# Column sums of a matrix on one core: the last 256 rows loaded as two one-row blocks, fewer matmuls, and every store issued from SyncE

## The chip, the cores and the metric

The kernel runs on one core of a Trainium2 chip. The metric is the device time of one execution in microseconds (us). The profile's span is about 1.9 us shorter than that time.

## The reference

```python
def setup_inputs():
    return {"x": np.random.randn(8192, 8192).astype(np.float32)}

def reference(x):
    return np.sum(x, axis=0)
```

## The kernel before

Pairs of rows, one pair to a partition, stream through three buffers of 64 KB per partition. VectorE adds row a and then row b of each pair to a running sum. The last two blocks of 256 rows are not added by VectorE: TensorE sums them over partitions with a matmul against ones, and adds the running sum in the same PSUM tiles. The last block comes in five column strips, so that little is left to do once the last bytes land.

```python
STRIPS = [[(2048, 4), (2048, 4)], [(2048, 4)], [(1024, 4)], [(512, 4)], [(512, 4)]]
...
    for t in range(n_blocks - 2):                       # 30 pairs
        xt = load_pool.tile([P, K, C], F32, tag="xt")
        nc.sync.dma_start(out=xt, in_=xr[t])
        a, b = xt[:, 0], xt[:, 1]
        if prev is not None:
            nc.vector.tensor_tensor(out=a, in0=a, in1=prev[:, 1], op=ADD)   # L81
        nc.vector.tensor_tensor(out=b, in0=b, in1=a, op=ADD)                # L82
        prev = xt
    ...   # near: a whole block; last: the block in five strips, two rows per partition
    for piece in pieces:
        column_sums(prev[:, 1], piece, True, False)
    for piece in pieces:
        for k in range(K):
            column_sums(near[:, k], piece, False, False)
    for piece in pieces:                                # each piece has its own PSUM tile
        s, c0, w, nj, n, ps, res = piece
        for k in range(K):
            column_sums(last[:, k], piece, False, k == K - 1)
        rows = 32 * nj
        nc.vector.tensor_copy(out=res[0:rows, :], in_=ps[0:rows, :])
        eng = nc.scalar if s == len(STRIPS) - 1 else nc.sync    # last store: ScalarE's queue
        eng.dma_start(out=..., in_=res[0 : 32 * (nj - 1) + 1 : 32, :])
```

Of the kernel before, what the change touches and what calls it, by code (L numbers as in the profile page):

```python
# [1 line left out]

# [4 lines left out]

F32 = mybir.dt.float32
ADD = mybir.AluOpType.add





STRIPS = [
    [(2048, 4), (2048, 4)],
    [(2048, 4)],
    [(1024, 4)],
    [(512, 4)],
    [(512, 4)],  # L20
]


@with_exitstack
def kernel(
    ctx: ExitStack,
    tc: tile.TileContext,
    x: bass.AP,
    out: bass.AP,
):  # L30
    nc = tc.nc
    P = nc.NUM_PARTITIONS
    R, C = x.shape
    K = 2
    assert R % (P * K) == 0
    assert sum(w for s in STRIPS for w, _ in s) == C
    n_blocks = R // (P * K)

    xr = x.rearrange("(b p k) c -> b p k c", p=P, k=K)

    const_pool = ctx.enter_context(tc.tile_pool(name="const", bufs=1))
    load_pool = ctx.enter_context(tc.tile_pool(name="loads", bufs=3))
    psum_pool = ctx.enter_context(
        tc.tile_pool(name="psum", bufs=1, space=bass.MemoryType.PSUM)
    )

    ones = const_pool.tile([P, 32], F32)
    nc.gpsimd.memset(ones, 1.0)  # L48

    pieces = []  # L50
    c0 = 0
    for s, strip in enumerate(STRIPS):
        for w, nj in strip:
            n = w // nj
            i = len(pieces)
            ps = psum_pool.tile([P, n], F32, name=f"ps{i}", tag=f"ps{i}")
            res = const_pool.tile([P, n], F32, name=f"res{i}", tag=f"res{i}")
            pieces.append((s, c0, w, nj, n, ps, res))
            c0 += w

    def column_sums(src, piece, start, stop):
        _, c0, w, nj, n, ps, _ = piece
        for j in range(nj):
            nc.tensor.matmul(  # L64
                out=ps[32 * j : 32 * j + 32, :],
                lhsT=ones,
                rhs=src[:, c0 + j * n : c0 + (j + 1) * n],
                start=start,
                stop=stop,
                skip_group_check=True,  # L70
            )



    prev = None
    for t in range(n_blocks - 2):
        xt = load_pool.tile([P, K, C], F32, tag="xt")
        nc.sync.dma_start(out=xt, in_=xr[t])  # L78
        a, b = xt[:, 0], xt[:, 1]
        if prev is not None:  # L80
            nc.vector.tensor_tensor(out=a, in0=a, in1=prev[:, 1], op=ADD)  # L81
        nc.vector.tensor_tensor(out=b, in0=b, in1=a, op=ADD)  # L82
        prev = xt


    near = load_pool.tile([P, K, C], F32, tag="xt")
    nc.sync.dma_start(out=near, in_=xr[n_blocks - 2])
    last = load_pool.tile([P, K, C], F32, tag="xt")
    t = n_blocks - 1
    c = 0  # L90
    for strip in STRIPS:
        w = sum(w for w, _ in strip)
        nc.sync.dma_start(out=last[:, :, c : c + w], in_=xr[t][:, :, c : c + w])  # L93
        c += w

    for piece in pieces:
        column_sums(prev[:, 1], piece, True, False)
    for piece in pieces:
        for k in range(K):
            column_sums(near[:, k], piece, False, False)  # L100
    for piece in pieces:
        s, c0, w, nj, n, ps, res = piece
        for k in range(K):
            column_sums(last[:, k], piece, False, k == K - 1)
        rows = 32 * nj
        nc.vector.tensor_copy(out=res[0:rows, :], in_=ps[0:rows, :])  # L106
        eng = nc.scalar if s == len(STRIPS) - 1 else nc.sync
        eng.dma_start(
            out=out[c0 : c0 + w].rearrange("(j i) -> j i", j=nj),
            in_=res[0 : 32 * (nj - 1) + 1 : 32, :],  # L110
        )


# [1 line left out]
_INS = ['x']  # L115
_OUTS = [((8192,), 'float32')]


# [23 lines left out]
```

## Time and profile before

| quantity | value | where it is read |
|---|---|---|
| time, median of 9 runs of one session | 629.1 us (628.85 to 629.36) | the runs |
| DMA engines busy with loads and stores | 99.1% of the span | page, DMA queues |
| one pair of rows (8.389 MB) | 19.31 us, 434 GB/s | timeline, from one first add to the next |
| VectorE's two adds of a pair | 2 x 8.69 us, then 1.89 us idle for data | timeline |
| end of the last copy to end of the span | 2.6 us | timeline |

These lines are from the page of the kernel before: the span, each engine's busy time, and the DMA queue that carries loads and stores with its packets, MB and share.

```profile
span 626.8 us, 698 instructions
PE 21.1 (3%) x240; PEld 7.8 (1%) x240; DVE 515.9 (82%) x65; POOL 0.3 (0%) x5
q1 hardware_dynamic: 5864, 268.47, 99.1%
```

The next lines are from the timeline of the kernel before. Columns are start, duration, engine, line, operation, out<-in, shapes and count; the bracket gives the engine's idle time before it and what ended it. An engine name with a q is a sequencer that issues a DMA.

```profile
573.04 8.69 DVE L82 TENSOR_TENSOR xt<-xt 128x8192 f32<-128x8192 f32 x1
583.63 8.69 DVE L81 TENSOR_TENSOR xt<-xt 128x8192 f32<-128x8192 f32 x1 [1.89 <-DMA xt<-in_x_dram]
592.35 8.69 DVE L82 TENSOR_TENSOR xt<-xt 128x8192 f32<-128x8192 f32 x1
601.15 6.54 PE L64 MATMUL ps<-xt,ones 128*32 128x512 f32 x48 [601.15 <-DVE xt L82]
...
622.26 0.51 SPq L108 DMA_DIRECT2D out_dram<-res  x1
622.93 0.50 SPq L108 DMA_DIRECT2D out_dram<-res  x1
623.17 0.64 PE L64 MATMUL ps<-last,ones 128*32 128x128 f32 x16 [0.62 <-DMA last<-in_x_dram]
623.88 0.29 DVE L106 COPY res<-ps 128x128 f32<-128x128 f32 x1 [0.98 <-PE ps L64]
624.20 1.08 ACTq L108 DMA_DIRECT2D out_dram<-res  x1
```

VectorE waits about 1.89 us for data in every pair from the third on (10.70 us in the second, at 41.93), so the DMA stream is the bound until the loads end. After that there is a chain: the last data, matmuls (0.64 us; a matmul is recorded as two passes), copy (0.29 us), and the store's issue (1.08 us on ScalarE's queue), its landing and the final waits.

### The profile page before, as it was taken

Reading aid. Unit: us, or ns where it says so; the run is one execution under the profiler, and the core shown is the slowest. Engines: PE = TensorE matmul, PEld = TensorE weight load, DVE = VectorE, ACT = ScalarE, POOL = GpSimd, SP = SyncE. Lnnn points to the kernel's source line nnn. Section 1 sums busy time; section 2 is a strip of 40 time slices with the busy share of each in tenths; the row PEclk is TensorE's granted clock in tenths of the full one; section 3 lists DMA queues with packets and bytes.
Section 4 is the critical chain, followed back from the end, with each engine's and each line's share of the span. In section 5 each row is a group of like instructions: output and inputs, shape, how many; then the busy total and the mean of one; then the engine's idle time right before and its main releaser. Section 6 shows DMA issues by size and latency. Waiting matters only on the chain.

```text
span 626.8 us, 698 instructions
## 1 busy us (share of the span) xinstructions
PE 21.1 (3%) x240; PEld 7.8 (1%) x240; DVE 515.9 (82%) x65; POOL 0.3 (0%) x5
## 2 busy tenths in 40 slices
PE   0000000000000000000000000000000000000067
PEld 0000000000000000000000000000000000000022
DVE  0538988889988889888898888988889988889831
POOL 0000000000000000000000000000000000000000
PEclk9999999999999999999999999999999999999999
DMA  9999999999999999999999999999999999999996
GB/s 402 406 464 402 468 402 468 402 468 402 468 402 468 402 468 402 468 402 468 402 468 402 468 402 468 402 461 410 448 422 435 435 422 448 422 448 422 448 400 273
DMA packets 5876, 268.52 MB, mean 428 GB/s; under 512 B 600, under 2 KB 612, under 8 KB 1392
## 3 DMA queue, kind: packets, MB, share of 16 engines
q1 hardware_dynamic: 5864, 268.47, 99.1%
q8 instruction: 2, 0.03, 0.0%
q14 instruction: 2, 0.02, 0.0%
q10 hardware_dynamic: 8, 0.00, 0.0%
HBM read 268.44 MB, written 0.03 MB: 428 GB/s over the span
## 4 chain that ended last, share of the span: by engine, by line
DMA 78%; DVE 21%; SPq 0%; issue 0%; PE 0%; DVEq 0%
DMA xt<-in_x_dram 73%; DVE xt L81 21%; DMA last<-in_x_dram 4%; SPq L93 0%; PE ps L64 0%; SPq L78 0%; DVEq L81 0%; DVE res L106 0%
## 5 line engine op out<-in xcount | busy, mean ns | idle before, releaser
L81 DVE TENSOR_TENSOR xt<-xt 128x8192 f32<-128x8192 f32 x29 | 252.1, 8692 | 64.7 <-DMA xt<-in_x_dram 64.7
L82 DVE TENSOR_TENSOR xt<-xt 128x8192 f32<-128x8192 f32 x30 | 260.7, 8692 | 23.5 <-DMA xt<-in_x_dram 22.5
L64 PE MATMUL ps<-xt,ones 128*32 128x512 f32 (+2 forms) x48 | 6.5, 719 | 601.1 <-DVE xt L82 601.1
L106 DVE COPY res<-ps 128x512 f32<-128x512 f32 (+2 forms) x6 | 3.1, 514 | 20.0 <-PE ps L64 20.0
L64 PEld LDWEIGHTS ps<-xt,ones 128*32 128x32 f32 x48 | 2.1, 154 | 605.3 <-issue 605.3
L64 PE MATMUL ps<-last,ones 128*32 128x512 f32 (+2 forms) x96 | 7.9, 454 | 1.5 <-DMA last<-in_x_dram 1.5
L64 PE MATMUL ps<-near,ones 128*32 128x512 f32 (+2 forms) x96 | 7.1, 450 | 0.0
L64 PEld LDWEIGHTS ps<-near,ones 128*32 128x32 f32 x96 | 3.0, 110 | 3.9 <-issue 3.5
L64 PEld LDWEIGHTS ps<-last,ones 128*32 128x32 f32 x96 | 2.6, 109 | 6.6 <-DMA last<-in_x_dram 4.1
L48 POOL MEMSET ones<- 128x32 f32 x1 | 0.1, 125 | 0.3 <-POOLq L126 0.3
L126 POOL MEMSET const-bfloat16-1.0<- 128x1 bf16 x1 | 0.1, 102 | 0.0
L126 POOL MEMSET const-uint8-127<- 128x1 uint8 x1 | 0.1, 102 | 0.0
L126 POOL MEMSET const-float32-0.0<- 128x1 f32 x1 | 0.1, 99 | 0.2 <-issue 0.2
L126 POOL MEMSET const-float32-1.0<- 128x1 f32 x1 | 0.1, 99 | 0.0
## 6 DMA issues: line engine op xcount, KB each, us to landing
last<-in_x_dram SPq DMA_DIRECT2D x1, 4096.0 KB
last<-in_x_dram SPq DMA_DIRECT2D x1, 2048.0 KB
last<-in_x_dram SPq DMA_DIRECT2D x1, 1024.0 KB
last<-in_x_dram SPq DMA_DIRECT2D x2, 512.0 KB, 27.8
xt<-in_x_dram SPq DMA_DIRECT2D x30, 29.8
out_dram<-res SPq DMA_DIRECT2D x3, 8.0 KB
near<-in_x_dram SPq DMA_DIRECT2D x1
out_dram<-res SPq DMA_DIRECT2D x1, 4.0 KB
```

The lines of the kernel that those rows point to most:

```text
L48: nc.gpsimd.memset(ones, 1.0)
L64: nc.tensor.matmul(out=ps[32 * j : 32 * j + 32, :], lhsT=ones, rhs=src[:, c0 + j * n : c0 + (j + 1) * n], start=start, stop=stop, skip_gro ...
L81: nc.vector.tensor_tensor(out=a, in0=a, in1=prev[:, 1], op=ADD)
L82: nc.vector.tensor_tensor(out=b, in0=b, in1=a, op=ADD)
L106: nc.vector.tensor_copy(out=res[0:rows, :], in_=ps[0:rows, :])
L126: nc = _bacc.Bacc("TRN2", target_bir_lowering=False, num_devices=1)
```

## The change

The intent is a shorter end: the last 256 rows become two blocks of one row per partition, the first added by VectorE (for three quarters of the columns), the second in strips. Each strip then has half the descriptors and half the matmuls, and the slower issue on ScalarE's queue (1.08 us in the trace of before, against 0.50 to 0.66 on SyncE's) is avoided. In the built program, 60 matmuls are left of 120 (the page counts two passes each).

```diff
-STRIPS = [[(2048, 4), (2048, 4)], [(2048, 4)], [(1024, 4)], [(512, 4)], [(512, 4)]]
+GROUP = 2048
+NQ, NJ, NI = 4, 4, 128
+STRIPS = [8, 4, 2, 1, 1]                       # in units of 512 columns
...
+    ps = [psum_pool.tile([P, 512], F32, ...) for g in range(n_groups)]    # 4 PSUM tiles
...
+    def finish(eng_copy, u0, nu):
+        g, q = divmod(u0, NQ)
+        words = slice(NI * q, NI * (q + nu))
+        eng_copy(out=res[g][:, words], in_=ps[g][:, words])
+        nc.sync.dma_start(out=outr[:, u0 : u0 + nu], in_=res[g][...])
...
+    for t in range(n_pairs):                   # 31 pairs; the last one's row b is not added
...
+    nc.sync.dma_start(out=near, in_=xn)        # one row per partition
+    for nu in STRIPS:                          # one row per partition, in strips
+        nc.sync.dma_start(out=last[...], in_=xl[...])
...
+    for g in range(n_groups):
+        column_sums(prev[:, 1], g * NQ, NQ, True, False)
+    g = n_groups - 1
+    column_sums(prev[:, 0], g * NQ, NQ, False, False)
+    for g in range(n_groups - 1):              # VectorE: near += row a of the last pair
+        nc.vector.tensor_tensor(out=near[:, cols], in0=near[:, cols], in1=prev[:, 0, cols], op=ADD)
+    g = n_groups - 1
+    column_sums(near, g * NQ, NQ, False, False)
+    for g in range(n_groups - 1):
+        column_sums(near, g * NQ, NQ, False, False)
+        column_sums(last, g * NQ, NQ, False, True)
+        finish(nc.scalar.copy, g * NQ, NQ)
+    u = sum(STRIPS[:2])
+    for nu in STRIPS[2:]:                      # three strips, all in PSUM tile 3
+        column_sums(last, u, nu, False, True)
+        finish(nc.vector.tensor_copy, u, nu)
+        u += nu
```

More of the change, by code (lines that the diff above doesn't have):

```diff
@@ L9 @@
 ADD = mybir.AluOpType.add
-STRIPS = [
-    [(2048, 4), (2048, 4)],
-    [(2048, 4)],
-    [(1024, 4)],
-    [(512, 4)],
-    [(512, 4)],
-]
+GROUP = 2048
+NQ, NJ, NI = 4, 4, 128
+STRIPS = [8, 4, 2, 1, 1]
 @with_exitstack
@@ L33 @@
     R, C = x.shape
-    K = 2
-    assert R % (P * K) == 0
-    assert sum(w for s in STRIPS for w, _ in s) == C
-    n_blocks = R // (P * K)
-    xr = x.rearrange("(b p k) c -> b p k c", p=P, k=K)
+    assert R % (2 * P) == 0 and C == 512 * sum(STRIPS)
+    n_pairs = R // (2 * P) - 1
+    n_groups = C // GROUP
+    xp = x[: n_pairs * 2 * P].rearrange("(b p k) c -> b p k c", p=P, k=2)
+    xn = x[n_pairs * 2 * P : R - P]
+    xl = x[R - P :]
+    outr = out.rearrange("(u j i) -> j u i", j=NJ, i=NI)
     const_pool = ctx.enter_context(tc.tile_pool(name="const", bufs=1))
@@ L48, with column_sums @@
     nc.gpsimd.memset(ones, 1.0)
-    pieces = []
-    c0 = 0
-    for s, strip in enumerate(STRIPS):
-        for w, nj in strip:
-            n = w // nj
-            i = len(pieces)
-            ps = psum_pool.tile([P, n], F32, name=f"ps{i}", tag=f"ps{i}")
-            res = const_pool.tile([P, n], F32, name=f"res{i}", tag=f"res{i}")
-            pieces.append((s, c0, w, nj, n, ps, res))
-            c0 += w
-    def column_sums(src, piece, start, stop):
-        _, c0, w, nj, n, ps, _ = piece
-        for j in range(nj):
+    ps = [
+        psum_pool.tile([P, 512], F32, name=f"ps{g}", tag=f"ps{g}") for g in range(n_groups)
+    ]
+    res = [
+        const_pool.tile([P, 512], F32, name=f"res{g}", tag=f"res{g}") for g in range(n_groups)
+    ]
+    def column_sums(row, u0, nu, start, stop):
+        g, q = divmod(u0, NQ)
+        v = row[:, u0 * 512 : (u0 + nu) * 512].rearrange("p (q j i) -> p j q i", j=NJ, i=NI)
+        for j in range(NJ):
             nc.tensor.matmul(
-                out=ps[32 * j : 32 * j + 32, :],
+                out=ps[g][32 * j : 32 * j + 32, NI * q : NI * (q + nu)],
                 lhsT=ones,
-                rhs=src[:, c0 + j * n : c0 + (j + 1) * n],
+                rhs=v[:, j],
                 start=start,
@@ L71, in column_sums @@
             )
+    def finish(eng_copy, u0, nu):
+        g, q = divmod(u0, NQ)
+        words = slice(NI * q, NI * (q + nu))
+        eng_copy(out=res[g][:, words], in_=ps[g][:, words])
+        nc.sync.dma_start(
+            out=outr[:, u0 : u0 + nu],
+            in_=res[g][0 : 32 * (NJ - 1) + 1 : 32, words].rearrange("j (u i) -> j u i", i=NI),
+        )
     prev = None
-    for t in range(n_blocks - 2):
-        xt = load_pool.tile([P, K, C], F32, tag="xt")
-        nc.sync.dma_start(out=xt, in_=xr[t])
+    for t in range(n_pairs):
+        xt = load_pool.tile([P, 2, C], F32, tag="xt")
+        nc.sync.dma_start(out=xt, in_=xp[t])
         a, b = xt[:, 0], xt[:, 1]
@@ L81 @@
             nc.vector.tensor_tensor(out=a, in0=a, in1=prev[:, 1], op=ADD)
-        nc.vector.tensor_tensor(out=b, in0=b, in1=a, op=ADD)
+        if t < n_pairs - 1:
+            nc.vector.tensor_tensor(out=b, in0=b, in1=a, op=ADD)
         prev = xt
-    near = load_pool.tile([P, K, C], F32, tag="xt")
-    nc.sync.dma_start(out=near, in_=xr[n_blocks - 2])
-    last = load_pool.tile([P, K, C], F32, tag="xt")
-    t = n_blocks - 1
-    c = 0
-    for strip in STRIPS:
-        w = sum(w for w, _ in strip)
-        nc.sync.dma_start(out=last[:, :, c : c + w], in_=xr[t][:, :, c : c + w])
-        c += w
-    for piece in pieces:
-        column_sums(prev[:, 1], piece, True, False)
-    for piece in pieces:
-        for k in range(K):
-            column_sums(near[:, k], piece, False, False)
-    for piece in pieces:
-        s, c0, w, nj, n, ps, res = piece
-        for k in range(K):
-            column_sums(last[:, k], piece, False, k == K - 1)
-        rows = 32 * nj
-        nc.vector.tensor_copy(out=res[0:rows, :], in_=ps[0:rows, :])
-        eng = nc.scalar if s == len(STRIPS) - 1 else nc.sync
-        eng.dma_start(
-            out=out[c0 : c0 + w].rearrange("(j i) -> j i", j=nj),
-            in_=res[0 : 32 * (nj - 1) + 1 : 32, :],
-        )
+    tail = load_pool.tile([P, 2, C], F32, tag="xt")
+    near, last = tail[:, 0], tail[:, 1]
+    nc.sync.dma_start(out=near, in_=xn)
+    u = 0
+    for nu in STRIPS:
+        nc.sync.dma_start(
+            out=last[:, u * 512 : (u + nu) * 512], in_=xl[:, u * 512 : (u + nu) * 512]
+        )
+        u += nu
[4 more added lines that the diff above has]
+    for g in range(n_groups - 1):
+        cols = slice(g * GROUP, (g + 1) * GROUP)
+        nc.vector.tensor_tensor(
+            out=near[:, cols], in0=near[:, cols], in1=prev[:, 0, cols], op=ADD
+        )
+    g = n_groups - 1
[8 more added lines that the diff above has]
+        finish(nc.vector.tensor_copy, u, nu)
+        u += nu
 _INS = ['x']
```

## The prediction

> **What bounds it now.** The page shows the DMA engines 99.1% busy, VectorE 82%, TensorE 3%. In the timeline the two adds of a pair take 2 x 8.69 us, then VectorE waits 1.89 us for data: one pair per 19.31 us, 8.389 MB / 19.31 us = 434 GB/s. [...] Buffers come free about 10 us before the queue would run dry. So about 617 of 626.8 us of span are a stream that the change leaves alone. Only the end can move.
>
> **The end before.** Timeline: last data reaches TensorE at 623.17; 8 matmuls (16 passes, 128 wide) to 623.88; copy 0.29; store issued on ScalarE's queue 624.20 to 625.28 (1.08 us); its packets are done at 625.53; span 626.77. Stores on SyncE take 0.50 to 0.66 us to issue.
>
> **Removed.** (a) Half the descriptors of the last 8 MB. Packets took 611 ns for 16 KB, 309 for 8, 159 for 4, 84 for 2: some 8 ns each beyond bytes. Estimated per engine: 19.73 us instead of 20.0, so data end 0.27 us earlier. (b) Four of eight matmuls of each strip: about 0.2 us. (c) Last store on SyncE: issue to data done 0.6 us instead of 1.33: 0.7 us.
>
> **Added.** (d) The last three strips share one PSUM tile, and the built program makes each strip's matmuls wait for VectorE's copy of the strip before: a series. Estimated from durations of before: matmuls 4x256 to copy 0.71, copy 0.42, matmuls 4x128 0.50, copy 0.29, matmuls 0.50, copy 0.29, handovers 0.12: 2.83 us from the first strip's start. (e) VectorE's add of pair 30 (602.9 to 611.6), then three 2048-column adds once the one-row block lands (612.7), estimated 2.29 us each, ending 615.0, 617.4, 619.7. TensorE then has near and last of groups 1 and 2, 0.86 us a group of four 512-wide matmuls at full clock, and reaches the strips at about 621.75, when the 1024-column strip lands (621.4 to 621.7). (f) ScalarE's copies and table load: off the path.
>
> **Sum.** 621.75 + 2.83 = 624.58 end of last copy, against 624.17; the SyncE store is done at 625.2, against 625.53. Gains of 1.2 us are mostly eaten by (d). Span about 626.45, time **628.7 us**, range **628.1 to 629.7**. Chance of faster by over 2%: 0.005; within 2%: 0.985; slower by over 2%: 0.01. (2% is 12.6 us, more than the tail.)
>
> **What would show it.** Timeline of the end: first matmul at 602.9, released by DMA, no longer VectorE; TensorE idle about 609 to 611.6; TensorE waiting for VectorE's copies between the last strips; last SyncE issue near 624.6, lasting 0.5 us. Last load 0.2 to 0.4 us earlier. Loop period unchanged.
>
> **What would make it wrong.** TensorE's clock. [...] cold groups of four took 1.71 us, full clock was granted from 607.03, and lost 3.65 us after the last matmul. The new schedule leaves TensorE about a quarter busy from 613.7 to 617.5; if that re-throttles it, groups cost 1.71 us and the end slips by up to 4.5 us (633 us, within 2%). Smaller: one DMA engine lagged the others by 0.75 us at landings; if that differs, the end shifts by tenths.

The named risk rests on what the trace of before shows, 1.71 us for a cold group and a clock lost at 627.51; that a stage a quarter busy could lose it too was the estimate. The 2.29 us of (e) is an estimate too; it can be worked out from the trace of before, where VectorE took 8.69 us for 8192 columns (an add) and 0.69, 0.42 and 0.29 us for 512, 256 and 128 (copies): 1.04 ns a column and 0.15 us. The trace of after shows 2.29 us. The table load of (f) took 1.28 us there, at 0.73 us of the span.

## More of the kernel before

The stage in dispute is only the last 25 us of about 629. So most traces are compared from one mark that all kernels share: the start of VectorE's first add of pair 29, the last event of the unchanged loop that both kernels have (583.63 us in the trace of before, 583.98 in that of after).

## The result and the profile after

The changed kernel takes 629.75 us (median of 6; 629.14 to 631.1), the kernel before 628.99 (median of 6; 628.69 to 629.2). The ratio is 1.0017 with an interval of 1.0004 to 1.003: same at 2%, but slower by 0.76 us in the medians and by about 1 us in the means, where 0.3 us faster had been forecast. The median lies 0.05 us above the stated range, and two of six executions, 631.1 and 630.99, lie far above it.

These are the lines of the page after that answer to those of before.

```profile
span 627.8 us, 469 instructions
PE 15.9 (3%) x120; PEld 4.0 (1%) x120; DVE 529.2 (84%) x66; ACT 3.0 (0%) x4; POOL 0.3 (0%) x5
q1 hardware_dynamic: 5416, 268.47, 98.9%
```

And these are from the timeline after.

```profile
583.98 8.69 DVE L85 TENSOR_TENSOR xt<-xt 128x8192 f32<-128x8192 f32 x1 [1.89 <-DMA xt<-in_x_dram]
603.34 5.85 PE L60 MATMUL ps<-xt,ones 128*32 128x512 f32 x32 [603.34 <-DMA xt<-in_x_dram]
612.04 1.94 PE L60 MATMUL ps<-xt,ones 128*32 128x512 f32 x8 [2.86 <-DVE xt L85]
...
617.55 4.93 PE L60 MATMUL ps<-tail,ones 128*32 128x512 f32 x48 [1.14 <-DVE tail L106]
...
622.55 0.42 DVE L72 COPY res<-ps 128x256 f32<-128x256 f32 x1 [2.85 <-PE ps L60]
622.72 1.20 SPq L73 DMA_DIRECT2D out_dram<-res  x2
623.02 0.43 PE L60 MATMUL ps<-tail,ones 128*32 128x128 f32 x8 [0.55 <-DVE res L72]
623.52 0.29 DVE L72 COPY res<-ps 128x128 f32<-128x128 f32 x1 [0.55 <-PE ps L60]
623.87 0.43 PE L60 MATMUL ps<-tail,ones 128*32 128x128 f32 x8 [0.41 <-DVE res L72]
624.03 0.54 SPq L73 DMA_DIRECT2D out_dram<-res  x1
624.36 0.29 DVE L72 COPY res<-ps 128x128 f32<-128x128 f32 x1 [0.55 <-PE ps L60]
625.07 0.52 SPq L73 DMA_DIRECT2D out_dram<-res  x1
```

Most of what the prediction said is here. The loop is unchanged (one idle time of about 1.89 us per pair). TensorE now starts when DMA releases it, at 603.34, and is idle for 2.86 us before 612.04. Between the last strips it waits for VectorE's copies (the releaser is DVE res L72), which is the predicted series. But between the end of the last copy, 624.36 + 0.29 = 624.65, and the issue of the last store, 625.07, there are 0.42 us that nobody had forecast.

One sign came out otherwise: the last load was to land 0.2 to 0.4 us earlier, and it landed 0.72 us earlier (39.49 us after the mark in the trace of before, 38.77 in that of after). Of the 16 landings of that strip, one for each DMA engine, the 14th hardly moved (38.14 and 38.11); what shrank was the lag of the slowest behind it (1.35 and 0.66 us). The end did not gain by it. TensorE was released at 617.55 by VectorE's add, worked through 48 passes, and came to the last strip at 623.87, when it had been there since 622.75.

Split at four events and counted from the mark, the two traces and the prediction (its absolute times minus the mark of the trace that it was made from) compare so. The packets' times come from the trace's own DMA records.

| us from the mark | before | after | predicted |
|---|---|---|---|
| last copy ends | 40.54 | 40.67 | 40.95 |
| last store is issued | 40.57 | 41.09 | 40.98 |
| its packets are done | 41.91 | 42.34 | 41.57 |
| span ends | 43.14 | 43.85 | 42.82 |

The changed end is 0.71 us longer: +0.13 to the last copy, +0.39 from copy to issue, -0.09 from issue to packets, +0.28 from packets to the end. Read against the prediction, the copy came 0.28 us earlier than forecast, and everything behind the copy came later: 0.39, 0.66 and 0.26 us.

### The profile page after: what moved, and what is told of

The parts are those of the page before. It is cut to its first block, busy times and chain, and to the rows that moved or that the text cites. A ratio compares the mean times of both kernels' runs of the same rounds, so it can differ in the third digit from the quotient of the medians.

```text
span 627.8 us, 469 instructions
## 1 busy us (share of the span) xinstructions
PE 15.9 (3%) x120; PEld 4.0 (1%) x120; DVE 529.2 (84%) x66; ACT 3.0 (0%) x4; POOL 0.3 (0%) x5
## 4 chain that ended last, share of the span: by engine, by line
DMA 76%; DVE 22%; PE 1%; issue 0%; SPq 0%; DVEq 0%
DMA xt<-in_x_dram 73%; DVE xt L85 21%; DMA tail<-in_x_dram 3%; PE ps L60 1%; DVE tail L106 1%; DVE res L72 0%; SPq L82 0%; DVEq L85 0%; DVEq L106 0%
## 5 line engine op out<-in xcount | busy, mean ns | idle before, releaser
L85 DVE TENSOR_TENSOR xt<-xt 128x8192 f32<-128x8192 f32 x30 | 260.8, 8692 | 66.8 <-DMA xt<-in_x_dram 66.8
L87 DVE TENSOR_TENSOR xt<-xt 128x8192 f32<-128x8192 f32 x30 | 260.8, 8692 | 23.7 <-DMA xt<-in_x_dram 22.7
L60 PE MATMUL ps<-xt,ones 128*32 128x512 f32 x40 | 7.8, 931 | 606.2 <-DMA xt<-in_x_dram 603.3
L60 PE MATMUL ps<-tail,ones 128*32 128x512 f32 (+2 forms) x80 | 8.3, 536 | 2.2 <-DVE tail L106 1.1
L106 DVE TENSOR_TENSOR tail<-tail,xt 128x2048 f32<-128x2048 f32 x3 | 6.7, 2287 | 1.0 <-DMA tail<-in_x_dram 1.0
L72 ACT COPY res<-ps 128x512 f32<-128x512 f32 x3 | 1.8, 586 | 618.9 <-PE ps L60 618.9
L72 DVE COPY res<-ps 128x128 f32<-128x128 f32 (+1 forms) x3 | 1.0, 336 | 4.0 <-PE ps L60 4.0
L60 PEld LDWEIGHTS ps<-tail,ones 128*32 128x32 f32 x80 | 2.3, 113 | 9.5 <-DVE tail L106 3.8
```

The source lines that it names most:

```text
L60: nc.tensor.matmul(out=ps[g][32 * j : 32 * j + 32, NI * q : NI * (q + nu)], lhsT=ones, rhs=v[:, j], start=start, stop=stop, skip_group_che ...
L72: eng_copy(out=res[g][:, words], in_=ps[g][:, words])
L106: nc.vector.tensor_tensor(out=near[:, cols], in0=near[:, cols], in1=prev[:, 0, cols], op=ADD)
```

## The experiments

Four theories: (A) the series of matmul and copy in the shared PSUM tile is what costs. (B) It is SyncE's queue that the last store waits for. (P), a sharper form of B that the first traces suggested: SyncE pauses at a fixed place of its instruction stream. (C) TensorE's clock makes the executions near 631. Each run has five timed executions; the kernel before has nine in each session (median 629.1 in the first, 628.88 in the second, 629.01 in the third). Each session ran on another chip, so medians are compared with the median of before in the same session: the first four runs below belong to the first session, the next four to the second, the last four to the third.

### The changed kernel again

No edit.

> The changed kernel unaltered, to see how its runs scatter beside those of before (so far 629.1 to 629.8, and two of six at 631.0). If the slow executions come from TensorE's clock (theory C), again about one in three lies 1 us or more above the others. If they were an accident of that session, all lie within 0.4 us of 629.7. The gap of 0.42 us between the last copy and the issue of the last store recurs if it belongs to the program.

Measured: 629.65 us median, 629.32 to 631.01; one of five was slow. From the mark, the last copy ended at 40.66, the store was issued at 41.08 and its packets were done at 42.33, each within 0.01 us of the first trace. The gap of 0.42 us belongs to the program, and so do the rare slow executions.

### A PSUM tile for each of the last strips (tests A against B)

```diff
+    own_ps = {u: psum_pool.tile([P, NI * n], F32, ...) for u, n in ((12, 2), (14, 1), (15, 1))}
+    def bank(u0, nu):
+        g, q = divmod(u0, NQ)
+        return own_ps[u0] if u0 in own_ps else ps[g][:, NI * q : NI * (q + nu)]
     def column_sums(row, u0, nu, start, stop):
+        if (u0, nu) == (12, NQ):
+            for u, n in ((12, 2), (14, 1), (15, 1)):
+                column_sums(row, u, n, start, stop)
+            return
...
-                out=ps[g][32 * j : 32 * j + 32, NI * q : NI * (q + nu)],
+                out=bank(u0, nu)[32 * j : 32 * j + 32, :],
```

> The changed kernel, with a PSUM tile of its own for each of the last three strips, so that no matmul waits for a copy. Theory A (the series matmul, copy, matmul, copy costs the time): the last copy ends near 623.8 instead of 624.65, TensorE's waits for res are gone, 0.6 to 0.9 us faster than the changed kernel. Theory B (the last store on SyncE is what costs, its queue and its 1.2 us from issue to data): the last copy ends earlier, but the last store's issue does not move by more than 0.2 us, since three stores of 0.6 us stand before it; under 0.3 us gained.

Measured: 629.78 us median (629.65 to 630.0), nothing gained. Two lines of its timeline say why.

```profile
623.78 0.29 DVE L83 COPY res<-own 128x128 f32<-128x128 f32 x1 [0.32 <-PE own L71]
625.22 0.52 SPq L84 DMA_DIRECT2D out_dram<-res  x1
```

The last copy ended at 624.07, 0.46 us earlier from the mark than in the changed kernel, and the store was issued 1.15 us after it, 0.26 us later from the mark than in the changed kernel. So B holds and A alone falls: SyncE was still issuing the stores before it, at 0.6 us each, and then paused.

Two details explain why the gain is nil. In the changed kernel SyncE has a chain of its own: from 622.72, when ScalarE's last copy lets it begin, it issues one store after another, and without the pause it would have been free near 624.67, when the last copy had just ended (624.65). The two chains are almost equally long, so shortening one of them gains nothing. And in this trace the loads landed later (the last packets at 39.04 us after the mark instead of 38.44), and with them ScalarE's last copy and the store behind it, by 0.26 us; that is the 0.26 us of the last store.

### The kernel before with its last store on SyncE (tests the prediction's term c)

```diff
-        eng = nc.scalar if s == len(STRIPS) - 1 else nc.sync
+        eng = nc.sync
```

> The kernel before, with only its last store moved from ScalarE's queue to SyncE's. The prediction's term (c) said 0.7 us faster (issue to data done 0.6 instead of 1.33 us). Read again, the traces say 1.2 us on SyncE: then the gain is 0.1 us at most, and with the gap of 0.4 us seen in the changed kernel it is 0.0 to 0.4 us slower.

Measured: 628.99 us median (628.7 to 629.12), against 629.1 for before; ratio 0.9997, interval 0.9984 to 1.0009.

```profile
624.12 0.29 DVE L106 COPY res<-ps 128x128 f32<-128x128 f32 x1 [0.96 <-PE ps L64]
624.44 0.50 SPq L108 DMA_DIRECT2D out_dram<-res  x1
```

The issue takes 0.50 us instead of 1.08, but the packets were done 1.23 us after its start (41.86 against 40.63 from the mark), where ScalarE's queue took 1.34. Moving the store is worth 0.1 us, not the 0.7 us of term (c).

### Matmuls that keep TensorE's clock (tests C)

```diff
+    idle = psum_pool.tile([P, 512], F32, name="idle", tag="idle")
+    def spin(row, c, n): ...   # n groups of four 512-wide matmuls into idle; the result is not used
...
+    spin(prev[:, 1], 0, 4)          # after the first 16 matmuls
+    spin(near, g * GROUP, 1)        # after near of group 3
+        if g == 0:
+            spin(near, 0, 1)        # after near of group 0
```

> The changed kernel plus 24 matmuls into an unused PSUM tile, placed in TensorE's idle stretches (after the first 16, after near of group 3, after near of group 0). Theory C (the clock falls back in the idle stretch and costs TensorE time before the strips): granted clock stays 1.0 from about 608 to the end, the slow executions near 631 vanish, the median is 0 to 0.3 us lower. If the clock has no part in the slow executions they stay.

Measured: 629.89 us median (629.68 to 630.08). No execution was slow, which is weak evidence by itself: if three in eleven are slow, as in the changed kernel, five in a row are fast in about one case of five. The median is not lower either. These are lines of the table of stretches: the stretch, its length, TensorE's busy time, its weight loads, VectorE, ScalarE, GpSimd, then the granted clock, the DMA share and GB/s. The stretches are those between which the clock changes: in the clock records of after its changes lie 3.413, 3.413 and 13.653 us apart, in those of before 20.48 us, all multiples of 3.413 us. First the changed kernel, then this one.

```profile
604.43:607.84 3.41, 3.41 (x20) 0.91 (x16) 3.41 (x1) 0.00 (x0) 0.00 (x0) 1.00 0.91 394
607.84:611.25 3.41, 1.35 (x12) 0.14 (x4) 3.41 (x1) 0.00 (x0) 0.00 (x0) 1.00 1.04 452
611.25:614.67 3.42, 2.62 (x16) 0.55 (x16) 2.41 (x2) 0.00 (x0) 0.00 (x0) 0.50 0.94 402
614.67:618.08 3.41, 2.17 (x24) 0.39 (x20) 3.41 (x3) 0.00 (x0) 0.00 (x0) 1.00 0.99 423
```

```profile
609.73:613.15 3.42, 3.42 (x36) 0.84 (x32) 2.41 (x2) 0.00 (x0) 0.00 (x0) 1.00 0.96 412
613.15:616.56 3.41, 2.94 (x31) 0.55 (x20) 3.41 (x2) 0.00 (x0) 0.00 (x0) 1.00 0.96 408
```

In the changed kernel a stretch of 3.41 us in which TensorE was busy for 1.35 us (40%) was followed by one at half clock. In this execution that was early enough to cost nothing: TensorE still stood idle for 1.14 us before VectorE released it at 617.55. With the extra matmuls the clock stays: 1.00 is granted in all five stretches from 606.32 to 623.39. That the median did not fall is not the clock's doing: the last load packets ended 39.26 us after the mark instead of 38.44. The DMA records show an instruction packet of 16 KB at 616.40, in the midst of the strips; in the changed kernel it comes at 621.88, when the loads are nearly done. Before has one at 612.34 and loads that end at 39.16. The own-tile kernels have it at 616.4 to 616.8 and loads nearly as late (38.98 to 39.10), but the last kernel below has one at 615.41 and its loads end at 38.44, so whether the packet is the cause stays open.

### The last store back on ScalarE's queue (tests B, and caught C)

```diff
-        nc.sync.dma_start(
+        eng = nc.scalar if u0 == C // 512 - 1 else nc.sync
+        eng.dma_start(
```

> The changed kernel, with only the last store moved back to ScalarE's queue. Theory B (SyncE's queue is what the last store waits for: 0.6 us for each store before it, and a pause of 0.43 us that every trace shows before SyncE's 80th recorded instruction, which here is the last store): the store is issued within 0.05 us of the last copy, at 624.8 instead of 625.2, its packets end 0.3 to 0.4 us earlier, span 0.3 to 0.5 us shorter. Theory A (the matmul and copy series alone is the bound): the last copy ends at the same 624.7 as in the changed kernel, and the store's time on either queue is the same, no gain.

Measured: 629.31 us median; three executions at 629.11 to 629.31 and two at 630.73 and 631.04. The three lie about 0.4 us below the changed kernel's, as theory B said, but part of that is the session: before was 0.22 us faster here than in the first. The surer sign is in the trace: from the last copy to the end of the span it took 2.73 us instead of 3.18. The profiled execution was one of the slow two, 631.04. First its table of stretches, then the end of its timeline.

```profile
607.83:611.25 3.42, 1.45 (x16) 0.24 (x8) 3.42 (x1) 0.00 (x0) 0.00 (x0) 1.00 1.06 460
614.66:618.07 3.41, 1.41 (x12) 0.32 (x16) 3.41 (x3) 0.00 (x0) 0.00 (x0) 1.00 0.95 406
618.07:621.49 3.42, 3.42 (x20) 0.87 (x16) 1.80 (x1) 0.36 (x1) 0.00 (x0) 0.50 0.99 402
```

```profile
626.23 0.29 DVE L72 COPY res<-ps 128x128 f32<-128x128 f32 x1 [0.55 <-PE ps L60]
626.55 1.08 ACTq L74 DMA_DIRECT2D out_dram<-res  x1
```

Here the stretch with 1.45 us of work (42%) was followed by one at full clock from 611.25, so TensorE did its next 16 passes in 1.97 us instead of 2.62, was done sooner, and had only 1.41 us of work (41%) between 614.66 and 618.07. Then the granted clock was 0.50 in the one stretch that is on the path: 20 passes were done there instead of 40. The last copy ended 42.36 us after the mark instead of 40.67, 1.69 us later. This shows theory C for one slow execution. The store itself went out 0.03 us after the copy, with no gap.

### Own PSUM tiles and the last store on ScalarE's queue

Both edits above together.

> Both edits: own PSUM tiles for the last strips, and the last store on ScalarE's queue. If the series and SyncE's queue each cost time but hide one another, the two together gain what neither gains alone: last copy at 624.0, issued at once, packets done near 625.4 instead of 626.4, 0.8 to 1.1 us faster than the changed kernel, that is 0.1 to 0.3 us faster than before. If only SyncE's queue matters, it gains no more than the previous run.

Measured: 629.54 us median (628.91 to 629.82), against 628.88 for before. The expectation was missed. The last copy ended at 40.29 and all packets were done at 41.75, 0.59 us earlier than in the changed kernel, but the span ended only 0.19 us earlier (43.66 against 43.85). SyncE waits for all stores at the end, and the pause had moved there.

### The first store on ScalarE's queue (tests P)

```diff
-        nc.sync.dma_start(
+        eng = nc.scalar if u0 == 0 else nc.sync
+        eng.dma_start(
```

> The changed kernel, with only the FIRST store (issued 5 us before the end, not on the path) on ScalarE's queue: SyncE has two instructions fewer ahead of its last store. Theory P (SyncE pauses 0.43 us at a fixed place of its instruction stream, the 80th recorded instruction): the pause moves behind the last store, into the final waits; last store issued near 624.8 instead of 625.2, span 0.3 to 0.45 us shorter. If the pause belongs to the last store itself (its wait, its queue's depth), it stays before it and nothing is gained.

Measured: 629.78 us median (629.12 to 630.43), against 628.88 for before.

```profile
624.61 0.29 DVE L72 COPY res<-ps 128x128 f32<-128x128 f32 x1 [0.55 <-PE ps L60]
624.93 0.51 SPq L74 DMA_DIRECT2D out_dram<-res  x1
```

The edit touches a store 4 us before the last one, yet the gap before the last store is gone (624.90 to 624.93), as P says. The packets were done 0.40 us earlier, but the span ended only 0.09 us earlier: the pause now stood behind SyncE's first final wait, where it costs the same. The half of the expectation about the place is right, the half about the span is wrong.

### Two more SyncE instructions in the kernel before (tests P)

```diff
         eng = nc.sync                                   # as in the run above
-    nc.sync.dma_start(out=near, in_=xr[n_blocks - 2])
+    for k in range(K):
+        nc.sync.dma_start(out=near[:, k], in_=xr[n_blocks - 2][:, k])
...  # and the first strip of last as two halves
```

> The kernel before with its last store on SyncE (as in the run e3_before_sync_last) and two more SyncE instructions: the load of near and the first strip of last are each issued as two halves. Theory P: its last store is now the 80th recorded instruction of SyncE, the pause of 0.43 us comes between the last copy and that store, and the span is 0.3 to 0.5 us longer than in e3_before_sync_last. If the pause belongs to the changed kernel's stores, there is none here before the last store and the span is that of e3_before_sync_last within 0.15 us.

Measured: 629.07 us median (628.74 to 629.5), against 628.88 for before in that session. The last copy ended 0.03 us before the store was issued, so the expected gap was not there. The trace shows the miscount: one more wait instruction had been built in, so the last store was the 81st. The pause stood before the 80th, a wait at 624.18, while SyncE had nothing to do until the copy ended at 624.45. The place agrees with P. The span did end 0.40 us later after the mark than in the run with the store alone on SyncE (43.54 against 43.14), within the expected 0.3 to 0.5, but by luck: 0.26 us of it came before the last copy ended (40.86 against 40.60) and 0.13 us from more final waits, none from the pause.

### Sixteen tiny loads early in the loop (tests P)

```diff
+    scratch = const_pool.tile([1, 64 * 16], F32, name="scratch")
...
+        if 5 <= t < 21:
+            nc.sync.dma_start(
+                out=scratch[:, 64 * (t - 5) : 64 * (t - 4)], in_=x[0:1, 64 * (t - 5) : 64 * (t - 4)])
```

> The changed kernel with 16 tiny loads (256 bytes, into an unused tile) issued from SyncE early in the loop, one behind each of 16 pair loads, so that SyncE's 80th recorded instruction falls in the loop or the strip loads, where SyncE has time. Theory P: no pause of 0.43 us before the last store nor in the final waits; last store issued 0.03 to 0.1 us after the last copy or the store before; span 0.35 to 0.5 us shorter than the changed kernel's (fast clock executions compared). If the pause belongs to the end of the program, it stays and nothing is gained. Executions with the clock lost near 618 (about 631) may still occur.

Measured: 629.37 us median (628.93 to 630.46), against 629.01 for before. Sixteen more DMAs, and yet the span ended earlier, 43.34 us after the mark instead of 43.85.

```profile
592.45 0.33 SPq L97 DMA_DIRECT2D tail<-in_x_dram  x1
593.22 0.33 SPq L100 DMA_DIRECT2D tail<-in_x_dram  x1
593.60 0.41 SPq L100 DMA_DIRECT2D tail<-in_x_dram  x1
...
624.11 0.29 DVE L72 COPY res<-ps 128x128 f32<-128x128 f32 x1 [0.55 <-PE ps L60]
624.42 0.52 SPq L73 DMA_DIRECT2D out_dram<-res  x1
```

The first three lines show where the pause went: the issue at 592.45 ends at 592.78 and the next begins at 593.22, 0.44 us later, while its successor follows after 0.06 us. The issue at 593.22 is SyncE's 80th recorded instruction. There it is harmless, since the queue still held about 10 us of loads (in the trace of after the load issued before this point landed at 603.20, 10.5 us after the issue at 592.70). The last store now goes out 0.02 us after the last copy (40.69 against 40.67 from the mark).

Over all 14 traces, the pause of 0.43 to 0.45 us stands just before SyncE's 80th recorded instruction, whatever that instruction is:

```
trace                        80th recorded instruction of SyncE    on the path?
before                       a final wait, before the last landing  no
before, store on SyncE       a final wait, before the last landing  no
after (both traces), own tiles, extra matmuls: the last store       yes
last store on ScalarE        a final wait, before the last landing  no
the same with own tiles      a final wait, after the last landing   yes
first store on ScalarE       a final wait, after the last landing   yes
one store                    a final wait, after the last landing   yes
two more instructions        a wait before the last copy ended      no
tiny loads (three kernels)   a strip load, 30 us before the end     no
```

This also answers two rivals: the pause is tied neither to a time (it begins between 592.78 and 627.53 us) nor to a number of DMAs (SyncE had issued 41 to 48 before it).

An 8 KB packet of the instruction queue 14 follows it in every one of them (at 625.74 in before, 625.71 in after), 0.6 to 0.9 us after the pause where the pause stands at the end, 3.6 to 5.1 us after it where it stands among the strip loads, with loads still running.

### Thirteen tiny loads (tests the order of the final waits)

The same edit with 13 instead of 16.

> The same with 13 tiny loads: the last store then uses the last of the eight DMA semaphores, the one that SyncE's final waits check last instead of first. Theory: in the changed kernel SyncE checks four more semaphores after the last landing, 0.065 us each; here all others are checked before it, so the time from the last store's packets to the end shrinks by 0.2 to 0.27 us on top of the previous run. If the order of the waits does not matter, the two runs are the same within 0.1 us.

Measured: 628.71 us median (628.53 to 629.02), against 629.01 for before. From the packets to the span's end it took 1.15 us instead of 1.39 with sixteen tiny loads, 0.24 us less, as expected; all earlier events agree within 0.01 us.

### One store for the last three strips

```diff
     # own PSUM tiles, as above
+        if 12 <= u0 < 15:
+            return
+        if u0 == 15:
+            u0, nu, words = 12, NQ, slice(0, 512)
```

> The changed kernel with own PSUM tiles for the last three strips and one store for all three, so that SyncE is free when the last copy ends. Last copy near 624.1, store issued within 0.05 us of it, packets done near 625.4; but SyncE's 80th recorded instruction is then among the final waits, so 0.4 us is lost there: 0.5 to 0.8 us faster than the changed kernel, about equal to before.

Measured: 629.06 us median (628.74 to 629.89), as expected about equal to before (629.01). The store went out 0.03 us after the copy (40.24, 40.21), the span ended at 43.30, 0.55 us before the changed kernel's, with the pause still among the final waits (626.28, after a wait that ended at 625.85).

### Everything that helped, in one kernel

Own tiles, one store, the extra matmuls, and 15 tiny loads.

> Everything that helped, in one kernel: own PSUM tiles, one store for the last three strips, 24 matmuls that keep TensorE's clock, 15 tiny loads that move SyncE's pause into the loop and put the last store on the semaphore checked last. Sum of the parts from the changed kernel's fast executions: 0.7 (series) + 0.4 (pause and queue) + 0.25 (final waits) = 1.1 to 1.4 us, so 0.3 to 0.6 us faster than before, and no execution near 631.

Measured: 628.61 us median (628.01 to 628.83), against 629.01 for before (628.25 to 629.45); ratio 0.9992, interval 0.998 to 1.0005.

```profile
623.36 0.29 DVE L83 COPY res<-own 128x128 f32<-128x128 f32 x1 [0.17 <-PE own L71]
623.67 0.54 SPq L88 DMA_DIRECT2D out_dram<-res  x1
```

From the mark: copy 39.65, issue 39.68, packets 41.07, end 42.23. That is 1.62 us earlier than the changed kernel and 0.91 us earlier than before in the profiled executions. Over all runs the gain on before is about 0.4 us by medians, and the interval still holds 1, so "faster than before" is likely but not established. The profiled execution, 628.01 us, was the fastest of the five. Thirteen tiny loads alone, without the other edits, came within 0.1 us of this kernel by medians (628.71).

## Why the prediction was wrong

**What bounds the kernel: right.** The stream is unchanged at one pair per 19.31 us, 434 GB/s in both traces. Only the end moved.

**Terms (b), (d), (e), up to the last copy: right, a little too dark; (a) was mis-sized, off the path.** The last copy was forecast for 40.95 us from the mark and came at 40.67. The loads ended 0.72 us earlier, not 0.27, and most of that was the lag of the slowest DMA engine and not the descriptors; the chain to the last copy ran through VectorE's adds and TensorE instead. The series of matmul and copy is in the timeline as forecast. But it is not what the result rests on: without it nothing was gained (own tiles, 629.78), because SyncE's queue was as long.

**Term (c) failed.** "Last store on SyncE: issue to data done 0.6 us instead of 1.33: 0.7 us." The measured value is 1.25 us in the changed kernel and 1.23 in the kernel before with the store moved, so the term is worth 0.1 us. The 0.6 fits a misreading: it is the time from the store issued at 622.93 to packets that ran from 623.41 to 623.53, but those were packets of the store issued at 622.26 (the 4 KB one; packets of 1 KB), done 1.27 us after its issue. The store issued at 622.93 was done at 624.16, after 1.23 us. The movement of its data was not in the recorded window of the issue: 0.50 us were recorded and 1.23 passed. The shorter issue bar seems to have been taken for a shorter store.

**Not in the prediction: the pause on SyncE.** It costs 0.39 us between the last copy and the last store. It stood in the trace of before too (624.51 to 624.94, among the final waits, before the last landing), where it was free. The change gives SyncE one load (31 pairs for 30) and one store more, each with its wait, so that the 80th instruction became the last store.

**Not in the prediction: the order of the final waits.** From packets to end it takes 1.51 us instead of 1.23. Of this 0.28 us, 0.16 lies behind the last landing (1.07 instead of 0.91), where SyncE has four waits left to check instead of one (626.83 to 627.05 in its records of after, 0.06 to 0.07 us apart). Thirteen tiny loads instead of sixteen, which give the last store another semaphore and leave all earlier events of the end as they were, took 0.24 us away there. The other 0.11 us lies between the packets and their landing (0.44 instead of 0.33) and is left open.

**The risk that was named, the clock, came true but was sized wrongly.** The prediction gave up to 4.5 us and treated it as unlikely; the range did not hold it. It came in three of eleven executions of the changed kernel, if all slow ones are of this kind, and cost 1.69 us in the one slow execution that was traced, of the kernel with its last store on ScalarE's queue. That the other slow executions have the same cause is argued from their time, not shown. The mean granted clock of each execution does not settle it: the slow three have 0.996, like the fast ones, and so would they by theory C, since the traced slow execution lost the clock for 3.41 us as a fast one does, only later. Two executions of other kernels at 630.43 and 630.46 have the lowest mean of all, 0.993, against 0.995 or more.

The sum: -0.28 (copy) + 0.39 (pause and queue) + 0.66 (term c) + 0.26 (from packets to the end, mostly the final waits) = +1.03 us against the forecast end, which turns a forecast of 0.32 us faster into the 0.71 us slower of the traces. The medians differ by 0.76. The spans of the two traces differ by more, 1.06 us, because the mark itself stood 0.35 us later in the trace of after than in that of before. This is within the wandering of the mark over all traces (583.56 to 584.23) and is left open. Why SyncE pauses at that place, too, is left open.

## What to carry to other kernels

When a tail of a few microseconds is tuned, follow the last store to its packets and to the final waits, and pair each store with its own packets by size, since neither the issue's bar nor the nearest packets tell what it costs. An issuing engine that handles several stores in the last microseconds (here SyncE, 0.6 us a store) can be the bound even where compute looks like it, and removing the compute series then gains nothing until the queue is shortened too (here 629.78 us with own tiles alone, 629.06 with one store as well). A gap without a waiting instruction may belong to a place in the instruction stream, as the 0.43 to 0.45 us did here: shift the stream by a few harmless instructions and see whether the gap moves.

## What the traces showed of the pause, the clock and the first packet

- SyncE's pause: 0.43 to 0.45 us before its 80th recorded instruction in 14 of 14 traces, followed by an 8 KB packet on queue 14. In the changed kernel 0.4 us of it stood openly on the path. No run here shows what it is.
- TensorE's clock fell after stretches of 3.41 us that were 40% and 41% busy (1.35 us in the trace of after, 1.41 in that with the last store on ScalarE's queue), stayed after one of 42% (1.45 us, in the latter), and came back after one of 77% (2.62 us, after). Yet in the trace of before, where 2.47 us of work lay between 600.20 and 603.62, four 512-wide passes still took 0.85 us up to 606.24, against 0.43 us from 607.50, so these figures give no threshold. The busy times rest on modelled ends of matmuls.
- In the trace of before the first packet of a 2 KB store began 1.14 us (SyncE, 622.93 to 624.07) and 1.24 us (ScalarE, 624.20 to 625.44) after the start of the issue; from the recorded end of the issue it was 0.64 and 0.17 us.
